# Hybrid encoder trunk on one Trainium2 core: the stages before attention in a written TensorE order, with weights loaded in smaller and earlier parts

## The chip, the cores and the metric

The kernel runs on one core of one Trainium2 chip. The metric is the device time of one execution in microseconds. The engines are named as in the profile: PE is TensorE's matmul side and PEld its weight loads, DVE is VectorE, ACT is ScalarE, POOL is GpSimd, SP is SyncE, which issues nearly all of the kernel's DMAs.

## The reference, cut to what matters

One layer over 1024 tokens of width 1024. A normed input is multiplied with one wide matrix `w_in`; three token mixers run on its columns, and a gated MLP with a short convolution follows.

```python
hn = rms_norm(x, norm_mix_g)
u_mla, u_fox, u_ssm, u_gate = split(hn @ w_in)

c_q, c_kv, k_rope = split(u_mla)                       # 384, 256, 32 columns
q  = (rms_norm(c_q, g) @ w_uq)                         # 8 heads x 96
kv = (rms_norm(c_kv, g) @ w_ukv)                       # 8 heads x (64 k + 64 v)
q = rope_tail(rms_norm(q, q_gain)); k = rope_tail(rms_norm([k_nope, k_rope], k_gain))
y_a = attention(q, k, v, chunk_mask) @ w_br_mla

q, k, v, f = split(u_fox)                              # 3 x 512, 8
q, k = rms_norm(q, g), rms_norm(k, g)                  # 8 heads x 64
y_b = attention(q, k, v, s + F_q - F_k) @ w_br_fox     # F = cumsum(log_sigmoid(f + b))

z, xBC, dt = split(u_ssm)
y_c = (rms_norm(ssd(silu(conv(xBC)), softplus(dt + b)) * silu(z))) @ w_br_ssm

x = x + (g0 * y_a + g1 * y_b + g2 * y_c) @ w_out       # g = sigmoid(u_gate + b_gate)
x = x + (silu(gate) * val) @ w_down                    # gate, val = conv(rms_norm(x) @ w_up)
```

## The kernel before, in words

Every float32 operand is split in two numbers, h and l (`split`, lines 130 to 135: ScalarE rounds a copy, VectorE subtracts it), and every product is made of three matmuls, h·h, h·l and l·h (`mm3`, line 165). Tokens are tiled by 128: there are eight tiles t, with 0 to 3 and 4 to 7 in the two halves of the normed, transposed input `hnh`/`hnl`.

The part before attention has these stages.

- Latents. `norm_tile` (line 180) norms a tile of x (VectorE and ScalarE; from tile 2 on POOL multiplies with the gain, `xg`) and has TensorE transpose it (`pt`, line 202). Then the products `cq` (24 matmuls of 384 columns, weights `w1`) and `ckv` (24 of 312, weights `w2`) follow, the norm of both (`cn`, line 400), and the latent's transposes (`tp`, line 407) into `ch`/`cl`. `wsplit` (line 346) loads a weight in pieces and splits it. `rope_and_columns` (line 227), called at tile 5, works out the sines and cosines on POOL and ScalarE and transposes small parameter columns (`pc_g`, `pc_f`, `pc_n`).
- MLA products. Per tile: `q` (18 matmuls of 384 columns), `kv` (12 of 512), the values split into `vv`, norms of the heads (`rq` is the factor), the rope (`rope`, lines 447 to 452, on POOL), then transposes of `qn` and `kn` (line 504), their split (`sh`, `sl`, lines 507 and 508) and the stores of `q_h`, `q_l`, `k_h`, `k_l`. Written after the eight tiles, but free to run among them, are the FOX values `fxv`: two halves of the columns with eight tiles each, a unit being 24 matmuls of 256 columns. `load_cols` (line 420) loads the weights of a half in four parts through two `raw` buffers.
- Chunks. Four blocks of 512 columns, in the order z's first half, FOX q, FOX k, z's second half; each is eight units `fx` of 24 matmuls of 512 columns. `load512` (line 622) loads a whole block's weights (`w5h`, `w5l`, two buffers in turns) in four parts. A z unit goes through tanh to `z_d`; a q or k unit through its norm (`fqn`, line 673), four transposes (line 677), `fsh`/`fsl` and a store. `gate_sums` (line 563), called ahead of the q block, forms the cumulated sums of the gates; `down_sums` (line 631) adds up columns of the last weight on POOL between units.
- Attention. 16 heads, two mixers by eight. TensorE's order there is written by hand: `merge` (line 837) interleaves scores, values and a fill of other products (`all_fill`, line 783, whose weights come by `fill_load`, line 745: ScalarE's `wh` and VectorE's `wl`, lines 750 and 751) by their estimated costs. It begins with `merge([], 8.0)` (line 1047), 8 us of fill alone; `load_head` (line 872) loads the four q and k tiles `qk0` to `qk3` of a head.

Ahead of attention a scheduler orders each engine's instructions by its own estimates, from what is ready; from attention on TensorE's order is fixed by `manual_schedule`. All DMAs named here stand in SyncE's one queue. SBUF pools opened later reuse the place of those closed before, and an instruction that writes a reused place waits for the last reader.

Of the kernel before, what the change touches and what calls it, by code (L numbers as in the profile page):

```python
# [16 lines left out]
ALU = mybir.AluOpType  # L17
# [25 lines left out]
def block_kernel(ctx: ExitStack, tc: tile.TileContext, x, positions, norm_mix_g, w_in, b_gate,  # L43
# [136 lines left out]
    def norm_tile(pool, tag, spool, psp, xt, gbc, h, l, t, ptag):  # L180
# [12 lines left out]
        if wide:  # L193
            A.activation(xn, xg, AF.Copy, scale=r)
        else:
            V.scalar_tensor_tensor(out=xn, in0=xt, scalar=r, in1=gbc, op0=ALU.mult, op1=ALU.mult)
        half, c0 = t // 4, (t % 4) * P
        for g in range(2):
            pt = psp.tile([P, 4, P], F32, name=uid("pt"), tag=ptag, bufs=2)
# [27 lines left out]
    def rope_and_columns(rp):  # L227
# [69 lines left out]


# [4 lines left out]
        pt = psp.tile([P, 84], F32, name="pcp", tag="tp", bufs=2)  # L303
        T.transpose(pt, pr, ident[0:84, 0:84])
        A.activation(pc_g, pt, AF.Copy, scale=0.5)
        for dst, srcs in ((pc_f1, (ffn_conv_w[:, 0, :], ffn_conv_w[:, 1, :])),
                          (pc_f2, (ffn_conv_w[:, 2, :], ffn_conv_b))):
            pr = rp.tile([88, P], F32, name=uid("pr_f"), tag="pr", bufs=1)
            for i, s in enumerate(srcs):
                SY.dma_start(pr[44 * i:44 * i + 44, :], s.rearrange("o (r p) -> (o r) p", p=P))  # L310
            pt = psp.tile([P, 88], F32, name=uid("pcp"), tag="tp", bufs=2)
            T.transpose(pt, pr, ident[0:88, 0:88])
            A.activation(dst, pt, AF.Copy)
        pr = rp.tile([NK, P], F32, name="pr_n", tag="prn", bufs=1)
        SY.dma_start(pr, ssm_norm_g.rearrange("o (r p) -> (o r) p", p=P))
        pt = psp.tile([P, NK], F32, name="pcn", tag="tp", bufs=2)
        T.transpose(pt, pr, ident[0:NK, 0:NK])
        A.activation(pc_n, pt, AF.Copy)
# [5 lines left out]
        for col, src, sc in ((fq_col, fox_q_gain, 0.125), (fk_col, fox_k_gain, 1.0)):  # L324
            SY.dma_start(col[0:64, :], src[0].rearrange("(p o) -> p o", o=1))
            SY.dma_start(col[64:128, :], src[0].rearrange("(p o) -> p o", o=1))
            if sc != 1.0:
                V.tensor_scalar_mul(col, col, sc)

    pmla = ExitStack()  # L330
    chp = pmla.enter_context(TP("chp", 1))
# [5 lines left out]
    cl = [chp.tile([P, 5, P], F32R, name=f"cl{t}", tag=f"cl{t}") for t in range(NT)]  # L337

    with ExitStack() as p0:
# [4 lines left out]
        gmix = None  # L344
# [15 lines left out]

        load_x(0)
        gmix = bcast(norm_mix_g[0], D, "gmix", ap_)
        norm_tile(ap_, "xn", mp, psp, xts[0], gmix, hnh, hnl, 0, "tp")
# [11 lines left out]
        for t in range(NT):  # L375
            if t + 3 < NT:
                load_x(t + 3)
# [1355 lines left out]
```

## Time and profile before

| What | us |
|---|---|
| Three runs | 2114.01, 2120.78, 2121.4 (median 2120.78) |
| Profiled execution | 2116.97 |
| Its span | 2115.3 |
| Latents (first products to the last) | about 9 to 97 |
| MLA products and FOX values | about 97 to 222.5 |
| Chunks | about 222.5 to 420 |
| First fill, entry of attention | about 420 to 438 |

The profiled execution stands 3.8 us below the median of the runs and within their range. Times are counted from the start of the span. A busy share says how long an engine worked; what a stage is worth is seen in the waits of the engine that bounds it. A row of a timeline gives start, length, engine, line, operation, output and inputs, shapes, how many equal ones follow (x) and in brackets the idle time before it with what ended it. The granted clock is the share of full speed that TensorE had in a stretch.

### The profile page before, as it was taken

What the parts mean: (1) busy time and instruction counts of PE and PEld (TensorE: products, weight loads), DVE (VectorE), ACT (ScalarE), POOL (GpSimd) and SP (SyncE); (2) the same over time, 40 slices, a digit from 0 to 9 for tenths busy, and PEclk for the clock granted to TensorE, in tenths of its full rate; (3) what the DMA queues carried; (4) which work ended last, traced back from release to release, by engine and by line L of the source; (5) the groups of instructions that cost most, each with busy time, mean ns of one, the idle gap of its engine ahead of it and who ended that gap; (6) DMA issues with size and microseconds to landing.
All of it is one profiled execution on the core that took longest, in us unless ns stands there. A gap on an engine that the chain in (4) does not pass through costs nothing.

```text
span 2115.3 us, 28991 instructions
## 1 busy us (share of the span) xinstructions
PE 2046.9 (97%) x10221; PEld 1686.4 (80%) x10221; DVE 1385.9 (66%) x2519; ACT 944.2 (45%) x1702; POOL 670.1 (32%) x678
## 2 busy tenths in 40 slices
PE   7999999999999999999999999999999999999999
PEld 6898787778888878887777788888778888877887
DVE  6687478356666667666777356557876776765664
ACT  5554222145555555555565223223544444444432
POOL 2454123222222222221342030000355445421855
PEclk9999999999999999999999999999999999999999
DMA  5168667564343543524442665341222222229665
GB/s 171 30 188 248 223 210 235 195 173 126 89 139 112 136 127 104 133 85 128 121 127 80 204 194 184 133 132 60 74 86 88 81 78 83 80 89 343 239 218 196
DMA packets 276650, 303.62 MB, mean 144 GB/s; under 512 B 19308, under 2 KB 209784, under 8 KB 276504
## 3 DMA queue, kind: packets, MB, share of 16 engines
q1 hardware_dynamic: 276504, 301.76, 46.1%
q8 instruction: 81, 1.33, 0.3%
q14 instruction: 65, 0.53, 0.1%
HBM read 209.03 MB, written 92.67 MB: 143 GB/s over the span
## 4 chain that ended last, share of the span: by engine, by line
PE 69%; ACT 3%; DVE 2%; POOL 2%; DMA 2%; issue 1%; SPq 0%; ACTq 0%; POOLq 0%; DVEq 0%
PE mm L800 16%; PE dn L1680 10%; PE ybr L171 9%; PE ua L1379 5%; PE uc L1379 5%; PE ud L1379 4%; PE wo L1424 4%; PE s L914 4%; PE tp L994 2%; PE ub L1379 2%; PE o L959 1%; PE o L967 1%; ACT pm L933 1%; DMA wr<-in_ffn_w_up_dram 1%; PE py L1190 1%
## 5 line engine op out<-in xcount | busy, mean ns | idle before, releaser
L800 PE MATMUL mm<-hnh,wh 128*128 128x512 f32 x576 | 240.0, 417 | 1.6 <-ACT wh L750 1.6
L940 POOL TENSOR_SCALAR pm<-pm,rs 128x128 f32<-128x128 f32 (+7 forms) x128 | 108.1, 847 | 405.5 <-DVE rs L939 269.6
L800 PE MATMUL mm<-hnh,wl 128*128 128x512 f32 x576 | 227.7, 395 | 0.5 <-DVE wl L751 0.5
L800 PE MATMUL mm<-hnl,wh 128*128 128x512 f32 x576 | 227.2, 395 | 0.0
L1680 PE MATMUL dn<-dr,dr 128*128 128x512 f32 x592 | 182.4, 389 | 0.0
L933 ACT ACTIVATE pm<-s,nmx 128x128 f32<-128x128 f32 (+2 forms) x192 | 110.2, 579 | 71.3 <-DVE nmx L930 57.1
L1680 PEld LDWEIGHTS dn<-dr,dr 128*128 128x128 f32 x592 | 111.1, 188 | 23.2
L800 PEld LDWEIGHTS mm<-hnh,wl 128*128 128x128 f32 x576 | 108.5, 188 | 26.0 <-DVE wl L751 1.0
L800 PEld LDWEIGHTS mm<-hnh,wh 128*128 128x128 f32 x576 | 109.3, 190 | 21.8 <-issue 3.8
L800 PEld LDWEIGHTS mm<-hnl,wh 128*128 128x128 f32 x576 | 109.2, 190 | 16.9 <-issue 0.2
L914 PE MATMUL s<-qk,qk 96*128 96x384 f32 (+5 forms) x480 | 118.4, 350 | 3.4 <-DMA qk<-q_h 2.0
L1000 DVE TENSOR_TENSOR ptl<-tp,pth 128x512 fp32r<-128x512 f32 (+1 forms) x160 | 98.8, 632 | 29.5 <-ACT pth L999 28.5
L1680 PE MATMUL dn<-dr 128*128 128x512 f32 x296 | 115.2, 389 | 0.0
L1475 POOL TENSOR_TENSOR S<-wr 128x512 f32<-128x512 f32 x20 | 26.8, 1341 | 268.2 <-DMA wr<-in_ffn_w_up_dram 237.0
L134 ACT ACTIVATE wh<-wr 128x1024 fp32r<-128x1024 f32 (+1 forms) x48 | 43.6, 908 | 150.6 <-PE ua L1379 66.1
L135 DVE TENSOR_TENSOR dr<-dr,dr 128x1024 fp32r<-128x1024 f32 x52 | 72.8, 1401 | 53.0 <-ACT dr L134 44.0
L171 PE MATMUL fx<-w5h,hnh 128*128 128x512 f32 x256 | 102.7, 406 | 3.5 <-ACT w5h L134 3.5
L999 ACT ACTIVATE pth<-tp 128x512 fp32r<-128x512 f32 (+1 forms) x160 | 84.0, 554 | 43.5 <-PE tp L994 43.2
L171 PE MATMUL fx<-w5h,hnl 128*128 128x512 f32 x256 | 102.7, 403 | 0.0
L171 PE MATMUL ybr<-ah,wh 128*128 128x512 f32 x256 | 100.5, 397 | 1.6 <-ACT ah L134 1.6
L171 PE MATMUL fx<-w5l,hnh 128*128 128x512 f32 x256 | 101.9, 399 | 0.0
L171 PE MATMUL ybr<-al,wh 128*128 128x512 f32 x256 | 101.5, 398 | 0.0
(464 smaller groups left out, 5818.9 us busy)
## 6 DMA issues: line engine op xcount, KB each, us to landing
dr<-act_d SPq DMA_DIRECT2D x99, 256.0 KB
wr<-in_ffn_w_up_dram SPq DMA_DIRECT2D x47, 512.0 KB
wr<-in_w_in_dram SPq DMA_DIRECT2D x36, 512.0 KB
g_d<-t SPq DMA_DIRECT2D x24, 512.0 KB
gl<-g_d SPq DMA_DIRECT2D x24, 512.0 KB
ws<-in_ffn_w_down_dram SPq DMA_DIRECT2D x22, 512.0 KB
wsum_d<-ws SPq DMA_DIRECT2D x22, 512.0 KB
act_d<-fa SPq DMA_DIRECT2D x22, 512.0 KB
```

The costliest lines, as they stand in the source:

```text
L134: i = A.activation(h, src, AF.Copy) if he is A else he.tensor_copy(h, src)
L135: return i, le.tensor_sub(l, src, f32(h))
L171: T.matmul(ps, a(k), b(k), start=(i == 0), stop=(i == n - 1))
L800: T.matmul(ps, a[:, k, :], b[half][:, k, :], start=(k == 0 and i == 0), stop=(k == NK - 1 and i == 2))
L914: T.matmul(ps[:, :w], q_[:, qs], k_[:, a:a + w], start=i_ == 0, stop=not last and i_ == len(o.passes) - 1)
L933: pss[cj][1][0] = later(0.9 + 0.1 * cj, lambda cj=cj, a_=a_, b_=b_: A.activation(p_[:, a_:b_], pss[cj][0][:, :b_ - a_], AF.Exp, bias=nb, a ...
L940: G.tensor_scalar(p_[:, 0:n * P], p_[:, 0:n * P], rs[:, 3:4], 0.0, op0=ALU.mult, op1=ALU.add)
L999: later(cs + 0.05, lambda th=th, pt=pt, off=off: A.activation(th[:, :off], pt[:, :off], AF.Copy))
L1000: pl[0] = later(cs + 0.6, lambda th=th, tl=tl, pt=pt, off=off: V.tensor_sub(tl[:, :off], pt[:, :off], f32(th[:, :off])))
L1379: T.matmul(ps, a, b, start=first and n == 0, stop=n == 11, skip_group_check=not first)
L1424: T.matmul(p, a, b, start=k == 0 and i == 0, stop=k == NK - 1 and i == 2)
L1680: T.matmul(ps[m], a[:, ts_], b[:, 512:], start=first_ and j == 0 and q == 0, stop=j == NFH - 1 and q == 2, skip_group_check=not first_)
```

## The change

The stages, products and outputs stay. These things differ:

- From the latents to the end of the chunks TensorE runs in the order in which the program is written (`order0`, after.py lines 339 to 824).
- `norm_tile` is parted into `norm_pre` and `norm_tp`. Per tile the order is `cq(t)`, transposes of tile t+1, `ckv(t)`, latent transposes of tile t-1 (those of tile 7 after the first `q`).
- `rope_and_columns` is parted: `rope_tables` is called at tile 1, and `columns` is a generator whose steps run from tile 2 on. The weights `uq` are loaded at tile 3 in a pool of their own.
- The MLA products go `q(t)`, a unit of FOX values, `kv(t)`, the q heads of tile t-1, another unit, the k heads of tile t-1; there is no first unit at tiles 0 and 5 and no second at tile 4. The second half's value weights are loaded at tile 4. Values get two `fv` buffers.
- Half (k 0 to 3) of the first chunk's weights is loaded at tile 5 into new tiles `w0h`/`w0l`, through the `raw` buffers of the value weights. After the last values six half units of that chunk follow, with the heads of tile 7 between them.
- The other weights come by `load_part`, a quarter every second unit one chunk ahead, split one quarter later; chunks 0 and 2 use `w0h`/`w0l` and `wh`/`wl` of the fill's pool, 1 and 3 `w5h`/`w5l`.
- The transposes of FOX q and k run two units late (`behind`); `fsh`/`fsl` get two buffers. `gate_sums` is a generator, one step per unit from the ninth on.
- Attention begins with `merge([], 5.0)`; heads with even number take their q and k tiles in `w0h`/`w0l`, the others in one set `qk0` to `qk3`.

```diff
+    order0 = tc.manual_schedule(engines={mybir.EngineType.PE})
+    order0.__enter__()
...
-            sq = mp.tile([P, 672], F32, name=uid("sq"), tag="sq", bufs=1)
+            sq = mp.tile([P, 416], F32, name=uid("sq"), tag="sq", bufs=1)
...
+        cols = columns(ap_)
+        for t in range(NT):
+            if t + 3 < NT:
+                load_x(t + 3)
+            if t + 2 < NT:
+                pre(t + 2)
+            if t == 1:
+                rope_tables(ap_)
+            th, tl = tok(hnh, t), tok(hnl, t)
+            p1 = acc("cq")
+            mm3(p1[:, :384], th, tl, lambda k: w1h[:, k, :], lambda k: w1l[:, k, :], NK)
+            if t == 0:
+                transposed(1)
+            elif t + 1 < NT:
+                transposed(t + 1)
+            p2 = acc("ckv")
+            mm3(p2[:, :312], th, tl, lambda k: w2h[:, k, :], lambda k: w2l[:, k, :], NK)
+            if t > 0:
+                latent(t - 1)
+            if t >= 2:
+                next(cols, None)
+            compressed(t, p1, p2)
+            if t == 3:
+                uqh, uql = wsplit(uqp, "uq", [P, 3, 768], [
+                    (k, c, c + 384, [(0, 384, uqv[:, k, c:c + 384])]) for k in range(3) for c in (0, 384)])
...
-            sqk = mp.tile([P, 8, 64], F32, name=uid("sqk"), tag="sqk", bufs=1)
+            sqk = mp.tile([P, 8, 96], F32, name=uid("sqk"), tag="sq", bufs=1)[:, :, 0:64]
...
+        for t in range(NT):
+            qn = q_part(t)
+            if t in (1, 2, 3, 4, 6, 7):
+                fox_values(next(fxv))
+            if t == 0:
+                latent(NT - 1)
+            if t == 4:
+                vcols.append(load_cols(fvp, "v", C_FQ + 1280, 256, 1))
+            qk[t] = kv_part(t, qn)
+            if t > 0:
+                heads_out(t - 1, qk[t - 1][0], gq_col, (q_h, q_l))
+            if t != 4:
+                fox_values(next(fxv))
+            if t > 0:
+                heads_out(t - 1, qk[t - 1][1], gk_col, (k_h, k_l))
+            if t == 5:
+                w0 = w0_tiles()
+                for k in range(4):
+                    raw = fvp.tile([P, 512], F32, name=uid("raw"), tag="vr", bufs=2)
+                    SY.dma_start(raw, w_inv[:, k, C_Z:C_Z + 512])
+                    split(w0[0][:, k, :], w0[1][:, k, :], raw)
+        for i in fxv:
+            fox_values(i)
...
+        fx_head = []
+        for t in range(6):
+            if t == 1:
+                heads_out(NT - 1, qk[NT - 1][0], gq_col, (q_h, q_l))
+            if t == 3:
+                heads_out(NT - 1, qk[NT - 1][1], gk_col, (k_h, k_l))
+            units = t
+            fx_head.append(fx_bank())
+            fx_part(fx_head[t], t, 0, 4, lambda k: w0[0][:, k, :], lambda k: w0[1][:, k, :])
...
+        def load_part(w, n, j, c0):
+            if n == 0:
+                raw = fpl.tile([P, 2, 512], F32, name=uid("raw"), tag="wr")
+            else:
+                raw = xp.tile([P, 2, 512], F32, name=uid("raw"), tag="raw", bufs=3)
+            SY.dma_start(raw, w_inv[:, 2 * j:2 * j + 2, c0:c0 + 512])
...
+            return lambda: split(*hl, raw)
...
-        for which in (3, 0, 1, 4):
-            if which == 0:
-                gate_sums()
-            c0 = (C_FQ, C_FQ + 512, C_FQ + 1024, C_Z, C_Z + 512)[which]
-            wh, wl = load512(c0)
+        for n, (which, c0) in enumerate(chunks):
+            wh, wl = getter(w, n, 0), getter(w, n, 1)
+            w = []
             for t in range(NT):
                 if units % 5 in (1, 3) and units // 5 * 2 + units % 5 // 2 < NFH:
                     down_sums(units // 5 * 2 + units % 5 // 2)
-                p = acc("fx", "mv" if units % 3 == 2 else "mm")
+                if n + 1 < len(chunks) and t % 2 == 0:
+                    parts_.append(load_part(w, n + 1, t // 2, chunks[n + 1][1]))
+                if len(parts_) > 1 or t == NT - 1 and parts_:
+                    parts_.pop(0)()
+                p = fx_head[t] if units < 6 else fx_bank()
+                fx_part(p, t, 4 if units < 6 else 0, NK, wh, wl)
                 units += 1
+                if len(behind) > 1:
+                    qk_out(*behind.pop(0))
...
+                    behind.append((out_qk(p), which, t))
+                if units >= 8:
+                    next(sums, None)
     pf.close()
     pjp.close()
+    order0.__exit__(None, None, None)
...
+        if (8 * br + h) % 2 == 0:
+            t = [e[:, i, :] for e in (w0p.tile([P, 2, S], F32R, name=uid(n), tag=n) for n in ("w0h", "w0l"))
+                 for i in range(2)]
+        else:
+            t = [pool.tile([P, S], F32R, name=uid(n), tag=n, bufs=1) for n in ("qk0", "qk1", "qk2", "qk3")]
...
-            merge([], 8.0)
+            merge([], 5.0)
```

More of the change, by code (lines that the diff above doesn't have):

```diff
@@ L452, in rope, with q_part @@
             eng.tensor_add(dst[:, :, 16:32], t3, t4)
[L454 to L455 removed]
+        def q_part(t):
             qn = mp.tile([P, 8, 96], F32, name=uid("qn"), tag="qn")
[L458 to L459 removed]
             for i in range(2):
@@ L514, in block_kernel @@
[L514 to L523 removed]
+            return qn, kn
@@ L524, in block_kernel @@
+        units = 0
     pmla.close()
@@ L650, in block_kernel @@
+        chunks = [(3, C_Z), (0, C_FQ), (1, C_FQ + 512), (4, C_Z + 512)]
+        w = [w0]
+        for j in (2, 3):
+            load_part(w, 0, j, C_Z)()
+        sums = gate_sums()
+        behind, parts_ = [], []
+        for n, (which, c0) in enumerate(chunks):
+            wh, wl = getter(w, n, 0), getter(w, n, 1)
+            w = []
             for t in range(NT):
```

246 lines of the change are left out of this document (137 added, 109 removed).

## The prediction

> **What bounds the kernel now.** I read the page's busy shares first, then busy time by stage, then TensorE's waits, then single stretches of the timelines. TensorE works 97% of the whole span; so only its waits and its clock in the part before attention, which the change rewrites, can move much. Busy time by stage (columns: stretch, length, busy time and count of PE, PEld, DVE, ACT, POOL, granted clock, DMA share, GB/s):
>
> ```profile
> PE 2046.9 (97%) x10221; PEld 1686.4 (80%) x10221; DVE 1385.9 (66%) x2519; ACT 944.2 (45%) x1702; POOL 670.1 (32%) x678
> ...
> 8.80:45.10 36.30, 29.99 (x153) 27.25 (x154) 26.01 (x99) 19.25 (x48) 7.17 (x3) 0.95 0.61 174
> 45.10:97.00 51.90, 50.43 (x334) 49.42 (x333) 32.32 (x142) 27.98 (x90) 26.54 (x57) 0.99 0.03 11
> 97.00:222.50 125.50, 113.57 (x761) 106.32 (x760) 101.10 (x267) 66.37 (x140) 51.72 (x120) 0.98 0.68 202
> 222.50:420.00 197.50, 192.24 (x853) 154.41 (x853) 115.69 (x301) 45.67 (x69) 58.21 (x44) 0.98 0.71 225
> 420.00:438.00 18.00, 12.84 (x50) 9.68 (x49) 3.50 (x5) 3.54 (x6) 0.37 (x1) 0.91 0.87 225
> ```
>
> The reader is to see where TensorE is idle: 6.3 us at the start, 1.5 in the latents, 11.9 in the MLA products (VectorE 81% busy), 5.3 in the four FOX/z chunks, 5.2 at the entry of attention. All of it together is 30 us of 2117: the room is small. What ended the waits (columns: waiting line, releaser, us in all, times, longest):
>
> ```profile
> PE tp L407 <- DVE cn L400: 6.5, 2, 3.8
> PE tp L677 <- DVE fqn L673: 5.2, 2, 3.2
> PE fxv L171 <- DVE fv L135: 4.5, 4, 2.3
> PE fx L171 <- ACT w5h L134: 3.5, 1, 3.5
> PE s L914 <- DMA qk<-q_h: 2.0, 1, 2.0
> PE mm L800 <- ACT wh L750: 1.6, 1, 1.6
> PE s L914 <- DMA qk<-q_l: 1.0, 1, 1.0
> PE q L171 <- DVE cn L400: 0.8, 1, 0.8
> PE tp L407 <- ACT pc_f L313: 0.7, 1, 0.7
> PE mm L800 <- DVE wl L751: 0.5, 1, 0.5
> PE tp L504 <- DVE sl L508: 0.5, 1, 0.5
> PE fxv L171 <- DVE v L135: 0.4, 1, 0.4
> PE fxv L171 <- DVE neg L583: 0.2, 1, 0.2
> ```
>
> A long wait costs twice: the clock drops to half behind it. Two such stretches, and one after a wait of 2.7 us (the second half of L407's 6.5) where it did not:
>
> ```profile
> 38.30:41.70 3.40, 3.28 (x12) 3.31 (x13) 3.07 (x16) 1.53 (x2) 0.77 (x1) 0.50 0.07 22
> 104.50:107.90 3.40, 3.40 (x18) 2.81 (x19) 1.98 (x6) 1.77 (x5) 1.63 (x9) 1.00 0.52 157
> 434.30:437.70 3.40, 3.11 (x8) 2.51 (x9) 0.46 (x2) 0.46 (x2) 0.37 (x1) 0.50 1.04 258
> ```
>
> 3.4 us at 0.50 lose 1.7. The stage's rows show such a stretch once in the latents' beginning, three times in the MLA products (mean clock 0.98 over 125.5 us), once in the chunks, once at the entry.
>
> **The change part by part.** The number of matmuls and transposes stays; SyncE gets two more loads. What differs is which instruction TensorE stands at when something is late: before, the scheduler may put any ready product there; after, the order is written out.
>
> *Start.* Tile 0's `ckv` now stands ahead of tile 1's `cq`:
>
> ```profile
> 33.28 0.55 PE L171 MATMUL ckv<-w2h,hnh 128*128 128x312 f32 x2 [0.46 <-ACT w2h L134]
> ...
> 38.42 0.88 PE L407 MATMUL tp<-ident,cn 128*128 128x128 f32 x3 [3.79 <-DVE cn L400]
> ...
> 44.98 0.33 PE L171 MATMUL cq<-w1h,hnl 128*128 128x384 f32 x1
> ```
>
> The last split of `w2` comes at 33.3 either way, and about 34.3 is the earliest that tile 0 is through. Before, TensorE had by 45.1 also done `cq` of tiles 1 and 2, `ckv` of tile 1, transposes of the next tiles and latent 0; it paid 3.79 and 1.7 behind. After, all but `cq(0)` and two transposes comes behind 34.3: that is some 15 us of work at full clock (48 `cq` and 24 `ckv` matmuls at 0.18 and 0.15, by the 384-column pace shown below, 20 transposes at 0.1, 0.8 for a last bit at half clock), ending near 49.3 instead of 45.1: **+4.2** (3.3 to 5.0).
>
> *Latents.* TensorE is busy 50.4 of 51.9 us, so another order wins and loses nothing while each latent finds its `cn` ready, which one tile's delay gives (24 times 0.18, eight transposes, 24 times 0.15: 8.8 us of work, where a wait of 3.8 was left before). Moved in among them: the rope tables to tile 1, ahead of the norms of tiles 4 to 7 on POOL, which with both is busy 26.5 us of this stretch and free for 25.4. The `uq` splits go to VectorE's 19.6 free us. Taken at **0**; without that cover one late norm costs like the start's wait, 3.8 and 1.7.
>
> *MLA products.* Per tile t TensorE runs `q`, a unit of FOX values, `kv`, heads of q of t-1, a unit, heads of k. The pace:
>
> ```profile
> 136.26 1.04 PE L504 MATMUL tp<-ident,qn 128*96 128x128 f32 x8
> 137.06 0.42 PE L171 MATMUL q<-uqh,ch 128*128 128x384 f32 x1
> ...
> 158.76 0.42 PE L171 MATMUL q<-uqh,ch 128*128 128x384 f32 x1
> 162.01 0.28 PE L171 MATMUL fxv<-v,hnh 128*128 128x256 f32 x1
> 162.13 0.28 PE L171 MATMUL fxv<-v,hnl 128*128 128x256 f32 x1
> 162.97 0.39 PE L171 MATMUL kv<-ukh,ch 128*128 128x512 f32 x1
> 163.20 0.40 PE L171 MATMUL kv<-ukl,ch 128*128 128x512 f32 x1
> ```
>
> `q` is 3.25 us, a unit 24 times 0.12 = 2.9, `kv` 12 times 0.23 = 2.8, eight transposes 0.8 and 0.1 for the switch. Against them stand two chains on other engines. The value weights come through two raw buffers:
>
> ```profile
> 109.95 0.68 ACT L134 ACTIVATE v<-raw 128x512 fp32r<-128x512 f32 x1
> 111.59 1.10 SPq L426 DMA_DIRECT2D raw<-in_w_in_dram  x2
> 114.44 0.63 ACT L134 ACTIVATE v<-raw 128x512 fp32r<-128x512 f32 x1 [0.90 <-DMA raw<-in_w_in_dram]
> 116.21 0.68 DVE L135 TENSOR_TENSOR v<-raw,v 128x512 fp32r<-128x512 f32 x1
> ```
>
> From the first split to the last subtraction 6.9 us, 2.85 of it a transfer. And a tile's heads, from the end of `kv` (tile 5):
>
> ```profile
> 156.06 0.39 PE L171 MATMUL kv<-ukh,cl 128*128 128x512 f32 x1
> 166.16 0.16 DVE L151 SCALAR_TENSOR_TENSOR rq<-rs_t,rq 128x16 f32<-128x16 f32 x1
> 166.47 2.46 POOL L498 TENSOR_TENSOR kn<-krr,rq 128x256 f32<-128x256 f32 x1 [3.02 <-DVE rq L151]
> 173.00 0.47 POOL L452 TENSOR_TENSOR qn<-rp,rp 128x128 f32<-128x128 f32 x1
> ```
>
> 17.0 us to the last rope instruction: 9.7 to the norm's factor, 7.2 on POOL.
>
> Tile 0: the splits of the first value weights stand on ScalarE behind `kv`'s evictions (two at 0.68), so `fxv(0)` ends no sooner than 1.4 + 6.9 = 8.3 after `kv`, 2.9 of it its own work: a wait of 5.4, 1.7 of clock behind it, and about 1.0 for latent 7, which now has `q(0)`'s 3.25 us as cover for a wait that was 2.7 to 3.8. Together 8.1.
>
> Ordinary tiles: between `kv(t)` and heads of q(t) stand two head groups, two units, `q` and `kv`: 1.8 + 5.8 + 3.25 + 2.8 = 13.65. The chain of 17.0 was measured with VectorE 81% busy with things that the scheduler had packed elsewhere; with the heads a tile later, 1.0 to 1.5 of splits fall out ahead of `rq`, and I take 15.5: some 1.8 for tiles 1, 2 and 6, the others covered by the wait before them. 5.4 (0 to 9).
>
> Tiles 4 and 5: here two units are left out of the order, and the second value weights and the first half of the first FOX weights (`C_Z`) are loaded through the same two raw buffers. Heads k(3) wait for ScalarE, behind the third value split, whose transfer starts two us after `kv(4)`: 2 + 2.85 + 0.7 + eviction, less 0.9 of heads q(3): 4.3. Between `kv(4)` and heads q(4) are then only 1.8 + 3.25 + 2.8 = 7.85 us of work, 12.2 with that wait; the chain runs about 5 longer than 15.5, because four `w0` splits stand ahead on ScalarE and VectorE until their loads land, two of them 2.85 apart. 15.5 + 4 - 12.2 = 7.2, and 1.7 of clock: 13.2 (8 to 17).
>
> Together 26.7. What goes: 2.7 + 0.8 + 0.7 + 4.5 + 3.5 + 0.5 + 0.4 + 0.2 = 13.3 of waits and 3 times 1.7: 18.4. Net **+8.3**. The wait for `w5h` (3.5) does go: half the weights lie ready, and the six half units of 2.8 us cover the rest.
>
> *Chunks.* Weights in quarters, one part ahead; transposes of q and k two units late, 11 us against a norm that missed its slot by 3.2 at most: 5.2 and 1.7 go, 0.5 remains (0 to 3) for the gate sums, whose steps now stand between units. **-6.4**.
>
> *Entry of attention.* Head 0's loads go to the FOX weight tiles, free some 45 us earlier, so 2.0, 1.0 and 1.7 go. `wh` and `wl` of the first fill stay (1.6 and 0.5): their splits stand behind the last tanh as before. **-4.7**. Three us less fill up front moves 12 matmuls into the heads: **0**, 3 either way.
>
> *Small edits*: two `fv` buffers instead of one are in the wait counted above; `sq` shared between q and k, `fsh`/`fsl` doubled, pools on other sides, two more loads in a stage with 32% DMA free: 0. Attention, SSD and FFN keep their order; memory places may move them 5 either way.
>
> Sum: 4.2 + 8.3 - 6.4 - 4.7 = +1.4 on the profiled execution's 2116.97, which is 3.8 below the median of the runs: **2118**. What tells from no change is 0.5%, 10.6 us: below 2110.2 or above 2131.4.
>
> The Trainium skill ("TensorE: Matmul & The Clock Gate", section "Part 1: The HAM clock gate") has the clock fall to half after at least one idle window of about 3.4 us, in free-running windows. The rows here differ: 0.50 after 2.0 + 1.0 at 434, full clock after 2.7 at 104. By the page the new waits of 5.4 and 7.2 would cost 1.7 each, as I took it, but the entry's 2.0 + 1.0 would have lost no clock, so 1.7 less could go there and the sum would be 2120. The trace shows the drop, so I keep 2118.
>
> **The rivals.** *The gains arrive in full* (35%). The new waits may be smaller than I build them, if the scheduler's order of ScalarE and VectorE lets weights' splits through between evictions, as it did at 109.95 and 114.44. Then the MLA products lose their 18.4 and gain little: 2117 + 4.2 - 18.4 - 6.4 - 4.7 = 2092; with half of tile 0's and tiles 4 and 5's waits left, 2103. For it: the order leaves the places of most of those 30 us. Against it: VectorE's 81%, and two raw buffers that take 6.9 us per set whichever order is written.
>
> *Every tile waits for its heads* (23%), the slower side. If the chain of 17.0 keeps its length, heads of q wait 17.0 - 13.65 = 3.4 at each of seven tiles, 23.5 instead of 5.4: 2136; with a clock drop behind two of them 2139. It decides from a chain of about 16 us upward. For it: the measured tile and VectorE's 81%. Against it: a wait at one tile leaves the next tile's chain the same time more, and TensorE's pause empties VectorE's queue.
>
> *The order does not change what TensorE does* because the scheduler had found it already: against this stand the 13.3 us of waits at places that the new order leaves; I give it no share of its own.
>
> **How the numbers follow.** Forecast 42%, 2118, its own range 2108 to 2129 from the bounds of start, ordinary tiles and tiles 4 and 5. The 35% of the first rival lie between 2092 and 2108, the 23% of the second between 2128 and 2139. The range 2094 to 2136 leaves out some 5% below and 10% above. Faster: the first rival and a bit of the forecast's lower edge, 0.37; slower: most of the second, 0.21; same: 0.42.
>
> **What the profile after would show.** Right: half clock at the first `fxv` and at heads q(4); waits of `tp` on `qn` in tiles 4 and 5; no wait of `fx` on `w5h` nor of `tp` on `fqn`; scores of head 0 not waiting for their loads; `ckv(0)` ahead of `cq(1)`, latent 0 done at about 49 against 45, and the last `fx` matmul ending near 426 against 420. Wrong: that end before 412 (first rival), a wait on `qn` at every tile (second), or a later phase moved by more than 5 us, for which nothing here gives a reason.

## The result and the profile after

The changed kernel takes 2142.01 us (median of four runs, 2134.55 to 2146.75) against 2120.76 before: a ratio of 1.0104, 95% interval 1.0067 to 1.0141. It is slower by 1%. The profiled execution took 2140.04 us with a span of 2138.3, 23.0 more than the span before.

Where the 23.0 us came from, by the starts of TensorE's instructions in the two traces:

| Stretch | before | after | difference |
|---|---|---|---|
| start to the first `q` | 96.0 | 108.9 | +12.9 |
| first `q` to the first `fx` | 126.6 | 134.6 | +8.0 |
| first `fx` to the last | 197.1 | 199.2 | +2.1 |
| last `fx` to the last `ybr` (attention, SSD) | 941.3 | 942.5 | +1.2 |
| last `ybr` to the end (FFN) | 754.4 | 753.1 | -1.3 |

Busy time by stage of the kernel after (columns as in the prediction: stretch, length, busy time and count of PE, PEld, DVE, ACT, POOL, granted clock, DMA share, GB/s); the last three rows are single stretches:

```profile
8.80:47.30 38.50, 32.37 (x149) 28.07 (x149) 27.23 (x87) 21.57 (x56) 23.85 (x45) 0.87 0.61 180
47.30:108.80 61.50, 53.42 (x337) 51.64 (x338) 38.24 (x161) 28.78 (x88) 11.95 (x16) 0.94 0.06 20
108.80:243.50 134.70, 117.58 (x745) 108.75 (x743) 90.55 (x237) 61.16 (x129) 51.30 (x119) 0.91 0.55 167
243.50:443.00 199.50, 193.47 (x871) 156.45 (x869) 123.23 (x326) 47.64 (x75) 59.86 (x46) 0.98 0.76 239
443.00:455.00 12.00, 9.83 (x48) 7.54 (x47) 4.63 (x9) 4.78 (x10) 1.35 (x3) 1.00 0.77 207
181.30:188.10 6.80, 5.35 (x22) 4.63 (x23) 3.87 (x12) 3.46 (x6) 0.69 (x2) 0.50 0.67 210
198.30:205.10 6.80, 5.48 (x26) 5.41 (x27) 5.20 (x18) 1.37 (x2) 2.23 (x5) 0.50 0.42 116
65.20:72.00 6.80, 4.62 (x15) 4.37 (x16) 5.19 (x25) 1.69 (x4) 1.26 (x2) 0.50 0.02 7
```

The latents, which had 1.5 us of idle TensorE in 51.9, now have 8.1 in 61.5 and a clock of 0.94. The MLA products' clock fell from 0.98 to 0.91: stretches at half clock are now up to 6.8 us long. Only the entry of attention is better. The waits of TensorE that answer to those of before:

```profile
PE tp L548 <- DVE rs_v L143: 6.3, 1, 6.3
PE tp L548 <- POOL qn L492: 6.3, 4, 2.7
PE tp L322 <- DVE cl L425: 4.1, 1, 4.1
PE tp L782 <- DVE fqn L776: 4.1, 1, 4.1
PE ckv L171 <- ACT w2h L134: 4.0, 2, 3.3
PE fxv L171 <- ACT v L134: 2.4, 2, 1.3
PE tp L782 <- DVE Fl L135: 1.9, 1, 1.9
PE mm L935 <- ACT wh L885: 1.6, 1, 1.6
PE tp L334 <- DVE rs_t L150: 1.4, 1, 1.4
PE tp L334 <- DVE cl L425: 1.4, 1, 1.4
```

Gone are the waits for `w5h`, for `fv` and for head 0's loads. New are waits at the transposes of the parameter columns (L322, L334), the heads' transposes (L548) and, still there though forecast as gone, `tp` for `fqn` (L782).

**The latents.** TensorE, ScalarE, VectorE and POOL around the longest of them (timelines of the kernel after):

```profile
62.56 0.71 PE L423 MATMUL tp<-ident,cn 128*128 128x128 f32 x5
67.38 0.40 PE L322 MATMUL tp<-ident,pr_g 84*128 84x84 f32 x1 [4.11 <-DVE cl L425]
...
62.81 1.15 ACT L194 ACTIVATE xn<-xg,nr 128x1024 f32<-128x1024 f32 x1 [1.82 <-DVE nr L151]
...
64.54 0.78 ACT L424 ACTIVATE ch<-tp 128x384 fp32r<-128x384 f32 x2
...
64.54 1.86 DVE L140 TENSOR_SCALAR rs_i<-v 128x2 int32<-128x2 int32 x1
...
66.78 0.55 DVE L425 TENSOR_TENSOR cl<-tp,ch 128x384 fp32r<-128x384 f32 x1
...
64.04 2.34 POOL L185 TENSOR_TENSOR xg<-xt,gmix 128x1024 f32<-128x1024 f32 x1 [7.06 <-ACT xn L194]
```

There are two `tp` banks (places in PSUM that a transpose is written to). The latent's transposes at 62.56 fill both, and the column transposes come next in the written order, so they need the split of the first (`ch`, then `cl`). ScalarE comes to `ch` at 64.54, behind the norm of a later tile; VectorE comes to `cl` at 66.78, after an instruction on two elements that took 1.86 us. That instruction ends at 66.40, and POOL's `xg`, begun before it, ends at 66.38. The same instruction at 56.99, with POOL idle, took 0.15 us. The Trainium skill ("SBUF — State Buffer", section "Who interferes with whom") says that VectorE and POOL share a pair of ports; where a VectorE instruction uses both of its pairs, as a `tensor_scalar` can, whichever engine issued first holds the shared pair for its whole instruction while the other stands still. The two ends, 0.02 us apart, agree.

**The chunks.** ScalarE and VectorE ahead of the wait of 4.08 us (timelines of the kernel after):

```profile
343.15 0.60 ACT L768 ACTIVATE fsq<-fx 128x512 f32<-128x512 f32 x1 [4.86 <-PE fx L606]
...
353.83 1.06 ACT L134 ACTIVATE w5h<-raw 128x1024 fp32r<-128x1024 f32 x1 [6.66 <-DMA raw<-in_w_in_dram]
354.79 0.58 ACT L768 ACTIVATE fsq<-fx 128x512 f32<-128x512 f32 x1
354.92 1.23 DVE L135 TENSOR_TENSOR w5l<-raw,w5h 128x1024 fp32r<-128x1024 f32 x1 [2.50 <-ACT w5h L134]
...
358.41 0.69 DVE L776 TENSOR_TENSOR fqn<-fx,fr 128x512 f32<-128x512 f32 x1
...
359.25 1.09 PE L782 MATMUL tp<-ident,fqn 128*128 128x128 f32 x4 [4.08 <-DVE fqn L776]
```

ScalarE stood 6.66 us at a split whose quarter had not landed, and VectorE 2.50 us at the same split's subtraction `w5l`. The `fqn` that TensorE waited for belongs to the unit whose squares `fsq` were taken at 343.15, ahead of that split; the last steps of its norm stood in VectorE's queue behind `w5l`. On ScalarE the next unit's squares, at 354.79, stood behind the split, though the product they need had ended at 349.1. The written order binds TensorE alone; on ScalarE the scheduler had drawn four splits of the next chunk together, ahead of the norms, and on VectorE their subtractions in among the norms' steps. The Trainium skill ("Perfetto Trace Analysis", section "Tensor Engine Instruction (MATMUL, LD_WEIGHTS)") notes that ScalarE and VectorE work strictly first in, first out; the idle 6.66 us with ready work behind it agree.

### The profile page after: what moved, and what is told of

Same layout as the page of the kernel before. It is cut to its first block, busy times and chain, and to the rows that moved or that the text cites. A ratio compares the mean times of both kernels' runs of the same rounds, so it can differ in the third digit from the quotient of the medians.

```text
span 2138.3 us, 28992 instructions
## 1 busy us (share of the span) xinstructions
PE 2057.1 (96%) x10221; PEld 1692.1 (79%) x10221; DVE 1390.2 (65%) x2521; ACT 946.6 (44%) x1704; POOL 671.1 (31%) x678
## 4 chain that ended last, share of the span: by engine, by line
PE 69%; DVE 3%; DMA 3%; POOL 2%; ACT 2%; issue 1%; POOLq 0%; ACTq 0%; DVEq 0%
PE mm L935 17%; PE dn L1820 10%; PE ybr L171 8%; PE ua L1519 5%; PE uc L1519 5%; PE ud L1519 4%; PE wo L1564 4%; PE s L1053 4%; PE tp L1133 3%; PE ub L1519 2%; DMA att_d<-o 1%; PE o L1106 1%; DMA wr<-in_ffn_w_up_dram 1%; PE o L1098 1%; PE py L1330 1%
## 5 line engine op out<-in xcount | busy, mean ns | idle before, releaser
L935 PEld LDWEIGHTS mm<-hnl,wh 128*128 128x128 f32 x576 | 109.4, 190 | 16.6 <-issue 0.5
L1139 DVE TENSOR_TENSOR ptl<-tp,pth 128x512 fp32r<-128x512 f32 (+1 forms) x160 | 97.8, 630 | 32.8 <-ACT pth L1138 31.7
L171 PE MATMUL ybr<-ah,wh 128*128 128x512 f32 x256 | 100.9, 399 | 1.6 <-ACT ah L134 1.6
L171 PE MATMUL ybr<-ah,wl 128*128 128x512 f32 x256 | 100.9, 397 | 0.0
L135 DVE TENSOR_TENSOR wl<-wr,wh 128x1024 fp32r<-128x1024 f32 (+1 forms) x48 | 68.3, 1423 | 37.5 <-ACT wh L134 28.7
L1067 DVE TENSOR_REDUCE nmx<-s 128x1 f32<-128x384 f32 (+3 forms) x128 | 65.8, 518 | 36.0 <-PE s L1066 34.5
L134 ACT ACTIVATE dr<-dr 128x1024 fp32r<-128x1024 f32 x52 | 55.2, 1062 | 73.8 <-PE dn L1820 41.3
```

What stands on the lines that cost most here:

```text
L134: i = A.activation(h, src, AF.Copy) if he is A else he.tensor_copy(h, src)
L135: return i, le.tensor_sub(l, src, f32(h))
L171: T.matmul(ps, a(k), b(k), start=(i == 0), stop=(i == n - 1))
L935: T.matmul(ps, a[:, k, :], b[half][:, k, :], start=(k == 0 and i == 0), stop=(k == NK - 1 and i == 2))
L1139: pl[0] = later(cs + 0.6, lambda th=th, tl=tl, pt=pt, off=off: V.tensor_sub(tl[:, :off], pt[:, :off], f32(th[:, :off])))
```

## The experiments

Times of one execution, unless a ratio is given. The stretches below are read from the traces and say more than the total, which differs between executions of one kernel by several us.

| Kernel | first `q` | first `q` to last `fx` | last `fx` to last `ybr` | time |
|---|---|---|---|---|
| before | 96.0 | 323.6 | 941.3 | 2116.97 |
| after | 108.9 | 333.8 | 942.5 | 2140.04 |
| e1_sched_latents | 102.8 | 342.2 | 943.3 | 2143.98 |
| e2_sched_all | 102.9 | 302.0 | 941.7 | 2102.47 |
| e3_cols_after_cq | 100.9 | 336.6 | 942.8 | 2135.28 |
| e4_sched_pin_uq | 99.6 | 299.5 | 945.4 | 2102.35 |
| e5_pin | 110.5 | 328.6 | 947.4 | 2143.14 |
| e6_pin_w0 | 111.4 | 335.2 | 945.5 | 2149.86 |
| e7_sched_fill8 | 103.5 | 298.8 | 938.2 | 2095.55 |
| e9_order_mended | 99.8 | 324.5 | 945.0 | 2125.26 |
| e11_heads_later | 101.0 | 325.0 | 950.3 | 2129.89 |
| e12_sched_best | 97.6 | 305.3 | 940.0 | 2098.54 |
| e13_sched_w0_late | 103.3 | 305.5 | 940.4 | 2105.03 |
| e14_sched_fv1 | 103.0 | 306.0 | 939.6 | 2104.39 |
| e15_heads_spread | 100.1 | 321.1 | 947.5 | 2123.83 |
| e16_sched_pinned | 97.7 | 298.4 | 941.7 | 2094.06 |
| e17_fill8 | 109.1 | 333.7 | 938.5 | 2136.8 |

The theory at the outset: it is the written order that costs the time, because it makes TensorE stand at work that is late elsewhere, while the moves themselves (early half, quarters, late transposes, buffers) are good. Its rival: the moves cost time by themselves.

### e2: no written order ahead of attention

```diff
-    order0 = tc.manual_schedule(engines={mybir.EngineType.PE})
-    order0.__enter__()
...
-    order0.__exit__(None, None, None)
```

> No written order ahead of attention at all; the moved loads, the late transposes, the quarters and the new memory places stay. If the written order is the whole loss, the time comes back to 2110 to 2122. If the moves cost by themselves, it stays above 2130. In between, the front stages' ends (108.9, 243.5, 442.7 in the changed kernel, 96.0, 222.6, 419.6 before) say which stage is which.

2102.47 us: 37.6 less than the changed kernel's execution and 13.4 less than the kernel before on the same chip (2115.9). The moves gain; the written order loses more. From the first `q` to the last `fx` it takes 302.0 us instead of 333.8 (323.6 before).

### e1: the scheduler's order in the latents alone

```diff
-    order0 = tc.manual_schedule(engines={mybir.EngineType.PE})
-    order0.__enter__()
     pmla = ExitStack()
...
+    order0 = tc.manual_schedule(engines={mybir.EngineType.PE})
+    order0.__enter__()
     pw0 = ctx.enter_context(ExitStack())
```

> The written TensorE order begins only at the MLA products; in the latents the scheduler orders TensorE as before the change, and all else of the change stays. If it is the written order that costs the latents their time, the first q moves from 108.9 us back to 97 to 99 and the kernel gains 10 to 12 us, to about 2127. If it is the moved work (rope tables at tile 1, uq splits among the latents, the new memory places), the first q stays later than 105 and the gain is under 4 us.

Neither case: the first `q` came at 102.8, half of the way back, with a new wait of 7.9 us for `cn` at 42; and the chunks had a wait of 12.4 us for `fqn`, so that the kernel took 2143.98. Under the scheduler's order 6.8 of the 12.9 us remain, so there something that was moved costs them (e4 and e12 say what). The chunks' wait depends on when transfers land: five kernels have one and the same order of TensorE, ScalarE and VectorE in the chunks, and the longer ScalarE stands at that split of `w5h`, the longer TensorE waits for `fqn`: 4.5 and 2.0 us in e17, 6.7 and 4.1 in the changed kernel, 7.4 and 8.8 in e6, 7.5 and 9.2 in e3, 10.9 and 12.4 in e1. Why the transfers land at other times is not shown.

### e3: the column transposes behind `cq`

```diff
+            if t >= 2:
+                next(cols, None)
             if t == 0:
                 transposed(1)
...
-            if t >= 2:
-                next(cols, None)
```

> The transposes of the parameter columns move from behind the latent's transposes to behind cq, one product earlier in the next tile; nothing else moves. If they wait only for the two tp banks that the latent has just filled, their waits of 4.1, 1.4 and 1.4 us and 2.3 us of half clock go: the first q at about 100, some 8 us less. If the chain of norms on VectorE, ScalarE and POOL sets the pace of the latents, the same waits turn up at the transposes of x, and the first q stays within 3 us of 108.9.

The first `q` came at 100.9, 8.0 us earlier, as the first case has it. TensorE's waits from 45 to 101 us in e3:

```profile
PE tp L322 <- DVE cl L425: 1.2, 1, 1.2
PE pt L206 <- ACT pc_f L335: 0.7, 2, 0.3
PE pt L206 <- DVE cl L425: 0.2, 1, 0.2
```

So 8.0 of the 10.7 us that the latents lost beyond the start were three small transposes in the wrong place: they stood where the two banks had just been filled. The total fell by 4.8 us alone, to 2135.28, since the chunks' wait for `fqn` was 9.2 us here.

### e5: the quarters' splits kept in program order

```diff
-            return lambda: split(*hl, raw)
+            return lambda: [tc.keep_in_program_order(e) for e in split(*hl, raw)]
```

> The splits of the chunks' weight quarters are kept in program order on ScalarE and VectorE, where the scheduler had drawn them ahead (four in a row); TensorE's order is the same. If the waits of the chunks (4.1 us for fqn, 1.9 for the gate sums, two stretches of half clock) come from splits that stand in the queues until their transfer lands, they go, and the chunks take about 190 to 192 us instead of 199.2: some 8 us less. If the norm chain of q and k is too long for two units, the waits stay within 2 us of what they are.

So marked, a split stays where the program has it, and the scheduler may not draw it ahead. Both waits went, and one of 2.5 us came at 398. The chunks took 194.7 us instead of 199.2: 4.5 of the 8. The total did not show it (2143.14), since the first `q` came 1.6 later and the stretch to `ybr` was 4.9 longer, neither of which the edit explains; one execution cannot carry a verdict of this size, the stage can.

### e4: no written order, `uq` splits in program order

```diff
                 uqh, uql = wsplit(uqp, "uq", [P, 3, 768], [
-                    (k, c, c + 384, [(0, 384, uqv[:, k, c:c + 384])]) for k in range(3) for c in (0, 384)])
+                    (k, c, c + 384, [(0, 384, uqv[:, k, c:c + 384])]) for k in range(3) for c in (0, 384)],
+                    tc.keep_in_program_order)
```

`wsplit` passes the two instructions of each split to its new argument.

> As e2 (no written order ahead of attention), and the splits of the uq weights keep their place in the program, at tile 3; in e2 the scheduler drew them to tile 1, ahead of the first latent's norm. If ScalarE standing at their transfers makes the wait of 8.6 us at 42 us, that wait falls under 2 us and with its half clock (10 us long) the kernel gains 8 to 10: 2093 or so. If the rope tables on POOL, now at tile 1, slow the norms on VectorE, the wait stays above 5 us and the time above 2099.

In between, so a miss: the wait at the first latent fell from 8.6 to 4.8 and the first `q` came 3.3 us earlier, but the total stayed, 2102.35, as the stretch to `ybr` was 3.7 longer. ScalarE had indeed stood at `uq` transfers there, with `cn` behind it (timeline of e2):

```profile
37.02 1.04 ACT L134 ACTIVATE uqh<-raw 128x384 fp32r<-128x384 f32 x2 [1.19 <-DMA raw<-in_mla_w_uq_dram]
38.23 0.53 ACT L134 ACTIVATE uqh<-raw 128x384 fp32r<-128x384 f32 x1 [0.16 <-DMA raw<-in_mla_w_uq_dram]
39.19 1.03 ACT L134 ACTIVATE uqh<-raw 128x384 fp32r<-128x384 f32 x2 [0.44 <-DMA raw<-in_mla_w_uq_dram]
```

### e6: the early half's splits kept in program order

```diff
-                    split(w0[0][:, k, :], w0[1][:, k, :], raw)
+                    for e in split(w0[0][:, k, :], w0[1][:, k, :], raw):
+                        tc.keep_in_program_order(e)
```

> The changed kernel with its written order; only the splits of the early half of the first chunk's weights keep their program place, behind the k heads of tile 4, where the scheduler had drawn them among tile 5's evictions. If these splits hold up the heads of q of tile 4, as the prediction says, the wait of 6.3 us at 199.6 falls to 1 to 3, and with the half clock behind it the last fxv comes 5 to 7 us earlier (at 237 instead of 243.4). If the chain of the heads itself is too long for the two units left out there, the wait stays above 5.

The wait at the q heads of tile 4 fell from 6.3 to 4.1, not to 1 to 3, and from the first `q` to the last `fxv` it took 132.8 us instead of 134.5. The splits are a third of that wait: it is 4.1 in e9 too, which keeps them in order, and 5.9 to 6.3 in e1, e3 and e5, which don't. The rest is something else; that it is the heads' chain is borne out by e15 below. The total was the worst of all, 2149.86: the first `q` came 2.5 us later, the chunks took 3.1 more with a wait of 8.8 for `fqn`, and what follows them 6 more, for which the edit gives no reason.

### e7 and e17: the first fill 8 us long again

```diff
-            merge([], 5.0)
+            merge([], 8.0)
```

e7 has this under the scheduler's order, e17 under the written one.

> As e2, with the fill ahead of attention 8 us long again instead of 5. Every kernel with 5 shows a wait of 2.9 us of py and a half clock of 7 to 10 us at the start of the SSD stage, which the kernel before doesn't have. If the shorter first fill shifts the interleaving there, wait and half clock go and the kernel gains 3 to 5: about 2098. If not (the new places of the tiles, say), the time stays within 2 us of 2102.5.

> The changed kernel with its written order and the first fill of 8 us instead of 5, nothing else. If the shorter fill costs what e2 and e7 say, the wait of py at the start of the SSD stage (2.9 us, with 6.8 us of half clock) goes, and from the last fx to the end of ybr it takes 938 to 939.5 us instead of 942.5. If it doesn't depend on the fill, it stays at 942 to 943.

Both as in their first case: 941.7 to 938.2 us from the last `fx` to the last `ybr` in e7, 942.5 to 938.5 in e17. The start of the SSD stage, waits of TensorE from 960 to 1210 us, first in the kernel after, then in e17:

```profile
PE py L1330 <- DVE y L1334: 2.9, 1, 2.9
PE stp L1275 <- ACT xT L1267: 2.1, 3, 0.7
```

```profile
PE stp L1275 <- ACT xT L1267: 1.4, 2, 0.7
PE py L1330 <- ACT E L1298: 0.5, 1, 0.5
```

The shorter first fill saves 3 us ahead of attention, but shifts how the fill falls between SSD's steps 560 us later, where it costs 3.5 to 4 us more than it saved. That wait of `py` is 2.9 us in all ten kernels with a fill of 5 us and 0.5 in all six with 8 us and in the kernel before. Its size in time is rougher: from the last `fx` to the last `ybr` kernels with the same fill differ by several us (941.7 to 950.3 with 5, 938.2 to 941.7 with 8). e7 is the fastest so far, 2095.55.

### e9: the written order, mended

The edits of e3, e4 (the `uq` splits), e5 and e6 together, with the written order.

> The written order with four mends: column transposes behind cq (as e3), and the splits of uq, of the early half and of the chunks' quarters kept in program order. By the single waits the gain is 8 in the latents, 5 to 7 at tile 5 and 4.5 to 8 in the chunks: 2118 to 2124, still above the 2102.5 of the scheduler's order. If the written order loses only by the weights' splits that stand ahead, it comes to 2105 or less; if it loses because the heads' and latents' chains are longer than the work between them, it stays above 2115.

2125.26, a little above the forecast and far above 2105. The latents are mended (99.8) and so are most of the chunks (192.4), but first `q` to last `fxv` is 132.0 us still. Waits of TensorE there:

```profile
PE tp L550 <- POOL qn L494: 10.6, 4, 4.1
PE fxv L171 <- ACT v L134: 2.9, 2, 1.6
```

### e11 and e15: the heads later

e11 is e9 with the q heads one unit of values later; e15 also moves the k heads behind the next tile's `q`.

```diff
             qn = q_part(t)
+            if t > 1:
+                heads_out(t - 2, qk[t - 2][1], gk_col, (k_h, k_l))      # e15 alone
...
-            if t > 0:
-                heads_out(t - 1, qk[t - 1][0], gq_col, (q_h, q_l))
             if t != 4:
                 fox_values(next(fxv))
+            if t > 0:
+                heads_out(t - 1, qk[t - 1][0], gq_col, (q_h, q_l))
```

> As e9 (written order, mended), with the heads of q one unit of FOX values (2.9 us) later, right ahead of the heads of k. If the work between kv and its heads was simply too short, by the 2.0, 2.8, 4.1 and 1.7 us that e9 waits there, these waits go but for some 1.2 at tile 4, and with their half clock the last fxv comes some 12 to 15 us after less time: stage from first q to last fxv 117 to 120 instead of 132.0, the kernel at 2110 to 2113. If the chain of the heads is stretched by whatever follows it (a wait moved is a wait kept), the stage stays above 127.

> As e11 (written order, mended, heads of q one unit of values later), and the heads of k no longer right behind them but behind the next tile's q. In e11 the heads of k wait 1.1 us each time, as they need the two tp banks that the heads of q have just filled. If the heads' distance and the two banks are the whole loss of this stage, it takes 117 to 120 us from first q to last fxv instead of 131.8 and the kernel 2113 to 2118. If VectorE, ScalarE and POOL cannot keep a period of 13.7 us a tile in this order, the stage stays above 127 whichever place the transposes have.

e11 missed: 131.8 us, no gain. Its waits of TensorE there:

```profile
PE tp L550 <- DVE sl L554: 9.1, 8, 2.1
PE tp L550 <- POOL qn L494: 3.3, 1, 3.3
```

The waits for `qn` fell to one of 3.3, but the k heads, now right behind the q heads, waited eight times for the two `tp` banks to be split (`sl`). e15 took 125.9 us, between its two cases. Its waits of TensorE from 100 to 230 us:

```profile
PE tp L550 <- POOL qn L494: 9.0, 2, 8.4
PE fxv L171 <- ACT v L134: 2.4, 2, 1.3
PE tp L550 <- DVE sl L554: 1.1, 1, 1.1
```

At the ordinary tiles the waits are gone, so the other engines do keep the period; the heads stood one unit and one product too early. What is left sits at two places: tile 0's values, and the q heads of tile 4, where the order leaves out two units (8.4 us). Each has a stretch of 6.8 us at half clock. The kernel took 2123.83: the chunks and the long stage to `ybr` did not follow, and it is still no match for the scheduler's order.

### e12, e13, e14: parts of the moves under the scheduler's order

e12 is e7 with the `uq` splits kept in program order and the rope tables at tile 5 again. e13 is e7 with the early half loaded behind the last value unit, e14 is e7 with one `fv` buffer.

```diff
-            if t == 1:
+            if t == NT - 3:                                             # e12
                 rope_tables(ap_)
...
-            if t == 5:
-
-                w0 = w0_tiles()
...
         for i in fxv:
             fox_values(i)
+        w0 = w0_tiles()                                                 # e13
+        for k in range(4):
+            raw = fvp.tile([P, 512], F32, name=uid("raw"), tag="vr", bufs=2)
+            SY.dma_start(raw, w_inv[:, k, C_Z:C_Z + 512])
+            for e in split(w0[0][:, k, :], w0[1][:, k, :], raw):
+                tc.keep_in_program_order(e)
...
-            vt = fvp.tile([P, 4, P], F32R, name=uid("fv"), tag="fv", bufs=2)
+            vt = fvp.tile([P, 4, P], F32R, name=uid("fv"), tag="fv", bufs=1)   # e14
```

> No written order ahead of attention, first fill of 8 us as e7, the uq splits kept in program order as e4, and the rope tables back at tile 5. If both the splits and the tables delay the first latent, the wait of 8.1 us that e7 has at 42.7 falls to some 1 to 4 as in the kernel before, the first q comes at 96 to 98 instead of 103.5, and the kernel takes 2087 to 2092. If the tables don't matter, the wait stays at e4's 4.8 and the time is 2092 to 2095.

> As e7 (scheduler's order, fill of 8), with the early half of the first chunk's weights loaded and split only behind the last FOX values. If the early half is what lets the chunks begin before the values end (fx from 207.8, fxv to 215.1 in e7), the wait for it comes back: 3 to 6 us more, 2099 to 2101. If the scheduler hides the loads anyway, the time stays within 2 us of 2095.6.

> As e7, with one fv buffer as before the change. If the second buffer is what takes the kernel before's 4.5 us of waits of fxv for fv and the half clock behind them away, they come back: 4 to 6 us more, 2099 to 2102. If the longer interleaving of values and MLA products leaves the store time enough, the time stays within 2 us of 2095.6.

e12: the first wait fell to 3.9 and the first `q` came at 97.6, as the first case says; the time is 2098.08 against 2117.78 before, ratio 0.9908 (0.9881 to 0.9934), and not 2087 to 2092, because a wait of 4.4 us for `fqn` came up in the chunks. The rope tables count a little too: e4, which moved only the splits, had kept 4.8 us of that wait and a first `q` at 99.6. e13 and e14 came out slower, as in their first case and 4 and 2 us beyond its numbers (2105.03 and 2104.39), but not for its reason: in e13 the wait for `w0h` is 1.1 us and in e14 none for `fv` came back, while both show waits in the chunks (4.0 for `fqn`; 2.3, 1.8 and 1.5) that e7 does not have. Four executions of e12 alone lie 8 us apart, so what the early half and the second buffer are worth by themselves stays open. ScalarE in e12 shows what stands in the chunks:

```profile
313.63 1.06 ACT L134 ACTIVATE w5h<-raw 128x1024 fp32r<-128x1024 f32 x1 [7.32 <-DMA raw<-in_w_in_dram]
```

### e16: the same with the quarters' splits kept in program order

The edits of e12 and e5, without the written order.

> As e12 (scheduler's order, fill of 8, uq splits kept, rope tables at tile 5), with the splits of the chunks' quarters kept in program order too. e12, e13 and e14 each show a wait of 4 us or so for fqn in the chunks, with up to 6.8 us of half clock, where e7 has 0.8. If these are splits drawn ahead of the norms and standing at their transfer, the wait falls below 1.5 us and the stretch from first q to last fx from 305.3 to 299 to 300: 2091 to 2094. If the wait is the norm chain's own, nothing moves by more than 2 us.

As in its first case: no wait for `fqn` is left, from the first `q` to the last `fx` it takes 298.4 us instead of 305.3, and the kernel 2093.43 us (2091.11 to 2094.99) against 2120.00 before on the same chip, ratio 0.987 (0.9849 to 0.9892). It is the fastest, 1.3% under the kernel before. Its stages and all waits of TensorE of 1 us or more behind 10 us, up to 460:

```profile
45.10:97.60 52.50, 50.17 (x329) 48.44 (x329) 36.35 (x142) 28.31 (x88) 26.20 (x57) 1.00 0.07 21
97.60:205.70 108.10, 105.78 (x743) 100.80 (x742) 88.86 (x240) 60.05 (x133) 48.26 (x114) 1.00 0.67 201
205.70:396.50 190.80, 190.77 (x876) 154.61 (x874) 127.46 (x330) 49.04 (x77) 59.76 (x51) 1.00 0.81 256
```

```profile
PE tp L422 <- DVE cn L411: 6.2, 2, 3.9
PE cq L171 <- ACT hnh L209: 2.2, 4, 0.8
PE mm L934 <- ACT wh L884: 1.6, 1, 1.6
PE ckv L171 <- ACT w2h L134: 1.1, 1, 1.1
```

In the chunks TensorE is busy 190.77 of 190.80 us at full clock, with the transposes late and the weights in quarters. The MLA products have 2.3 us idle in 108.1.

## Why the prediction was wrong

The forecast was 2118 us, no change; measured were 2142.01, above its range of 2094 to 2136. On the profiled executions the sum was to be +1.4 us and is +23.0, a miss of 21.6. By its own steps:

- *Start*, +4.2 (3.3 to 5.0): `ckv(0)` was through at 33.05, not 34.3, and what the kernel before had done by 45.1 was done at about 47.3, but for four transposes (some 0.4 us). +2.2: the place was right, the size half.

```profile
33.05 0.52 PE L171 MATMUL cq<-w1h,hnh 128*128 128x384 f32 x1
...
46.84 0.33 PE L171 MATMUL cq<-w1h,hnl 128*128 128x384 f32 x1
47.76 0.33 PE L206 MATMUL pt<-ident,xn 128*128 128x128 f32 x1 [0.58 <-DVE nr L141]
```

- *Latents*, 0: **this step failed.** They lost 10.7 us (12.9 less 2.2). The prediction weighed each latent against its `cn` and found 8.8 us of cover, which was right: the only wait of a latent for `cn` is one of 0.7 us, of tile 7, behind the first `q`. It did not count the column transposes as users of the same two banks. e3 returned 8.0 us by moving them alone. It also named a price for a late norm (3.8 and 1.7) that would have been half of the loss.
- *MLA products*, +8.3: first `q` to first `fx` is 8.0 longer, and the heads of tile 7 (1.8 us) have moved behind it: 9.9. The sum held, by luck: its parts erred by nearly the same in both directions. Waits were 16.6 us where 23.3 were forecast (value weights 2.7 instead of 5.4, tiles 4 and 5 9.7 instead of 11.5); half clock lasted 23.8 us, in which TensorE was busy 19.8, a loss of 9.9 where two stretches of 1.7 were counted. At tiles 4 and 5 two terms did not follow from the prediction's own figures: 2 + 2.85 + 0.7 - 0.9 is 4.65 before the eviction is added, not 4.3, and a chain said to run 5 us longer was entered with 4. The 4.3 forecast at heads k(3) came as 2.7 at heads q(3) and 0.7 at heads k(3). The places named, tile 0, the ordinary q heads and tile 4, are those that e15 and e9 show.
- *Chunks*, -6.4: **this step failed.** They gained nothing: 199.2 us instead of 197.1, 1.8 of it the moved heads. (One half-clock stretch that the prediction has going from the MLA products, 222.6 to 226.0, lies behind the first `fx`; counted here, the miss is larger by its 1.7.) The prediction took 11 us of lateness against a norm that had missed its slot by 3.2, and forgot what it had priced at tiles 4 and 5 itself: a split that the scheduler draws ahead stands in the queues of ScalarE and VectorE until its transfer lands, and the norm behind it. e5 and e16 show that these are the waits, and the five kernels under e1 that they grow with the time that the split stands.
- *Entry of attention*, -4.7: from the last `fx` to the first `o` it takes 24.7 us instead of 32.8, 8.1 less, of which the shorter fill is 3. Right, and so were the two waits said to stay (1.6 and 0.5).
- *Shorter fill*, 0, 3 either way: it cost 4.0 us net by e17. The bound was too narrow, and the place (SSD) was not foreseen.

So 10.7 and 6.7 us of the miss are the latents and the chunks, 4 the fill, and the other steps nearly cancel. The first rival, the gains in full, had priced the stages from MLA to the chunks at 18.4 + 6.4 = 24.8 us; e16 has 25.2 there (323.6 less 298.4). So gains of that sum were to be had, under the scheduler's order and with the splits kept in program order; which move brought which part is not shown. With the written order they were lost again: the prediction's comparison, which put it as "any ready product" against an order written out, was right in kind and too mild in size. The second rival gave about the measured time, 2136, but by a mechanism (a longer chain at every tile) that is not what missed: the MLA stage came out within 2 us of the forecast.

## What to carry to other kernels

An order written for one engine is only as good as the order of the engines that feed it: here the scheduler went on drawing weight splits ahead of norms on ScalarE and VectorE, and one whose transfer had not landed held up the norms behind it; keep such instructions in program order before writing an order on TensorE. Here that alone was not enough: with it the written order took 2125.26 us (e9), since some instructions still stood too close behind what they need. When instructions are moved, count their buffers (here two PSUM banks) as well as their inputs. Read each change stage by stage from the trace: in one execution the totals hid gains of 4 to 8 us that the stages showed plainly.

## What the runs showed of the hardware

Half clock lasted longer than in the kernel before, where each stretch ahead of attention was 3.4 us: 6.8 us at 0.50 around waits of 2.7 and 0.7 us (181.3 to 188.1), and 10.2 us around waits of 3.3 and 0.7 (24.2 to 34.5). The length of a wait did not decide it alone. In the changed kernel one of 2.1 us had 3.4 us of half clock (150.5 to 153.9), and in the kernel before two of 0.7 and 0.8 us had it (96.3 to 99.7), while one of 2.7 us, ending at 104.4, had none. The waits for the first fill's weights, 1.6 and 0.5 us in both, were followed by half clock in e16 (400.1 to 403.5) and by none in the kernel before. The Trainium skill ("TensorE: Matmul & The Clock Gate", section "Part 1: The HAM clock gate") asks for an idle window of about 3.4 us; these waits are shorter, so the trace does not agree. In the MLA products the clock lost 9.9 us beside the waits' 16.6.
